# Two heads of an RWKV recurrence as one block on TensorE, and key norms repeated by transposes

## Chip, cores and metric

The kernel runs on one core of one Trainium2 chip. The metric is the device time of one execution in microseconds (us); lower is better. All arithmetic is in float32; the large products split each operand into a high and a low float32r part and add three products.

## What is computed

One residual block of a streaming encoder on 1024 frames of width 1024: half a SwiGLU feed-forward network (FFN 1, hidden width 2816), a mixing layer of two head groups, and half of FFN 2, each after an RMS norm that is scaled and shifted by a modulation vector (`silu(c) @ w_ada + b_ada`). The mixing layer projects each frame; group A (8 heads of 64) is the RWKV-7 recurrence, group B (8 heads of 64) is attention of 64-frame chunks over a band of nine chunks. Both outputs go through `w_out`.

The recurrence, per head and frame (state is 64 x 64):

```
sa    = state @ (-kk)                     # kk: the removal key, k * k_k, divided by its norm
state = state * w + sa (x) (kk * a) + v (x) k
y     = state @ r
```

The kernel computes it in chunks of 64 frames: inside a chunk the frame-to-frame dependence is a triangular system, whose inverse (TT) is computed ahead; between chunks only the state passes on.

## The kernel before

The frames are two halves (A, B) of 512. Everything is issued by a planner at build time: tasks are Python generators that say what they wait for, and a model clock of the engines decides which task issues its next instructions. Products of the large matrices ("mains") have the lowest priority and fill TensorE whenever no background task is ready; their weights are streamed through four staging buffers (`wst`), split by ScalarE (`whi`) and VectorE (`wlo`). The order of the mains is: FFN 1 of A, projection of A, FFN 1 of B, output projection of A (`oA`, which needs the recurrence rA and the attention of A), projection of B, FFN 2 of A, output projection of B, FFN 2 of B. The recurrence and attention of A run as background beside FFN 1 of B, those of B beside FFN 2 of A.

`spawn_rwkv` (L1549) makes, for a half, two groups of two head pairs. Each group is one task that prepares its two pairs one after the other (`rwkv1`, L1203) and then inverts their triangles (`inverse`, L1363); then the two recurrences (`rwkv2`, L1386) run as two tasks beside each other. The second group starts when both recurrences of the first are done.

`rwkv1` loads the shifted projections (`shift`), makes decay products `gp` and their inverse `gi`, the norms `rk` of the removal keys per head and frame, and spreads these norms over channels: L1259 to L1262 multiply a broadcast column of `rk` with the identity, eight matmuls into 64-row halves of a bank (`rkb`). It builds `RA` (r and -kk with decays) and `BKB` (kk*a, k and again kk*a, with inverse decays; head 1 reads its last two, so that head 1 has its rows in swapped order), the masked products `GA` and `GR`, and `BKn`, the transposed `BKB`. `GA`, `GR` and `BKn` are one tile per head, in the sixteen slots of the half's set, which at other times hold the normalised input.

`rwkv2` first finishes the inverse (`qb`, `ub`), then goes through eight chunks (L1440). `UV` (per head: the state's rows and the values, on opposite halves of the partitions for the two heads) is loaded ahead of it. Each chunk has three TensorE steps, each of two matmuls with 64 moving columns, one for each head: `px` (L1444), `pu` (L1454) and `pz` (L1461). VectorE copies `X` out of `px`; ScalarE and VectorE copy `pu` into `UV`, one head each; VectorE adds `pz` to the decayed state, twice 64 rows into the next chunk's `UV` and once 128 rows into `Z`. After the chunks `yb` gives the outputs, which are normalised per head, gated, transposed (`tb`) and written to `mix`, from where the output projection reads them as `mx` (L1579).

In the trace every matmul has line L512, every transpose L516 and every other recorded operation L172 (helpers), so groups are told by tile names. A float32 matmul leaves two records, a transpose one.

Of the kernel before, what the change touches and what calls it, by code (L numbers as in the profile page):

```python
# [245 lines left out]
class Builder:  # L246
# [113 lines left out]
    def setup(self):  # L360
# [3 lines left out]
        self.sets = [self.pool("set0", 16), self.pool("set1", 16)]  # L364
# [54 lines left out]
    def setup2(self):  # L419
# [26 lines left out]
        for p in range(4):  # L446
            nc.gpsimd.memset(self.Zc[p], 0.0)
        dp = self.dp
# [78 lines left out]
    def ada_first(self, v):  # L527
# [5 lines left out]
        def load(i, v=v):  # L533
            q, kb = steps[i]
            n = 2 if (v, q) in ADA_PE else 2 if v or kb in (0, 3) else 3
            w[v, i] = self.tile(self.sets[1], "n1", 16, "wa", [P, 2, 256], reads=n)
            nc.sync.dma_start(w[v, i], self.a["w_ada"][v, :, 2 * kb : 2 * kb + 2, q * 256 : q * 256 + 256])
# [63 lines left out]
    def ada(self, vs):  # L601
# [5 lines left out]
        def load(i):  # L607
            v, cb, k = steps[i]
            w[i] = self.tile(self.sets[1], "n1", 16, "wa", reads=1)
            nc.sync.dma_start(w[i], self.a["w_ada"][v, :, k, cb * H : cb * H + H])  # L610
# [92 lines left out]
    def norm_first(self):  # L703
# [18 lines left out]
        for q in range(4):  # L722
# [3 lines left out]
            for d in two:  # L726
                yield scale(d), back(d), xr[d], "th"
                nh.append(self.tile(self.sets[0], "n0", 16, "nh", dt=F32R))
# [3 lines left out]
            for d in two:  # L732
                yield t[d % 2], "n0"
                nl.append(self.tile(self.sets[0], "n0", 16, "nl", dt=F32R))
                nc.vector.scalar_tensor_tensor(nl[d], xr[d], scale(d), t[d % 2], op0=OP.mult, op1=OP.subtract)
                if d == 0:
                    self.n["n1A"] = nh, nl

    def norm(self, key, hf, j, src=None):
        nc = self.nc  # L740
        s = self.sets[hf]
# [12 lines left out]
        nh, nl, vs = [], [], []  # L754
# [6 lines left out]
        def low(d):  # L761
            nc.vector.scalar_tensor_tensor(nl[d], vs[d], scale(d)[1], nh[d].bitcast(F32), op0=OP.add, op1=OP.subtract)

        def step(d, x):
            yield x, rstd, "th", f"n{hf}", lambda: 0.0 if len(self.mains) < 2 else self.clock.at["vector"]
            sc, sh = scale(d)
# [3 lines left out]
            nh.append(self.tile(s, f"n{hf}", 16, "nh", dt=F32R))  # L770
            nl.append(self.tile(s, f"n{hf}", 16, "nl", dt=F32R))
# [373 lines left out]
    def tb(self, hf, name, shape=None):  # L1145
        return self.tile(self.sets[hf], f"n{hf}", 16, name, shape)
# [56 lines left out]
    def rwkv1(self, hf, p):  # L1203
# [36 lines left out]
        rk = self.sm("rk", [P, 8], 2, reads=10)  # L1240
# [39 lines left out]
        nc.scalar.activation(BKB[:, :, 2], BKB[:, :, 0], AF.Copy)  # L1280
# [8 lines left out]
        GR, GA, BKn = [], [], []  # L1289
        for h in range(2):  # L1290
            yield f"n{hf}"
            GR.append(self.tb(hf, "GR", [P, NC, C]))
            yield f"n{hf}"
            GA.append(self.tb(hf, "GA", [P, NC, C]))
        half = [slice(0, 64), slice(64, 128)]
        for c4 in range(2):
            yield BKB, RA, self.two
            gb = [self.bank("gb", 2) for h in range(2)]
            for i in range(4):
                c = 4 * c4 + i  # L1300
                for h, s in enumerate(half):
                    self.mm(
                        gb[h][:, i * P : i * P + P],
                        BKB[s, c, h : h + 2].rearrange("p k t -> p (k t)"),
                        RA[s, c].rearrange("p k t -> p (k t)"), side=2,
                    )
            for h in range(2):
                g4 = gb[h].rearrange("p (c k t) -> p c k t", c=4, k=2)
                for k, o in ((1, GA[h]), (0, GR[h])):
# [7 lines left out]
        for c in range(NC):  # L1317
            for h, s in enumerate(half):
                self.tp_(
                    bt[h][:, c * C : c * C + C],  # L1320
                    BKB[s, c, h : h + 2].rearrange("p k t -> p (k t)"),
                    self.ident[s, s], side=2,
                )
        for h in range(2):
            yield f"n{hf}"
            BKn.append(self.tb(hf, "BKn", [P, NC, C]))
            nc.scalar.activation(BKn[h], c3(bt[h]), AF.Copy)
# [8 lines left out]
        for h in range(2):  # L1336
            yield GA[h]
            for b in range(2):
                q = h * 64 + b * 32
                w = (4 * i + 2 * h + b) * 8  # L1340
                nc.sync.dma_start(nd[w : w + 8].rearrange("c s t -> s c t"), GA[h][q : q + 32, :, b * 32 : b * 32 + 32])
        return dict(p=p, RA=RA, GR=GR, GA=GA, BKn=BKn, bon=bon, gC=gC)

    def inverse(self, hf, st):
# [26 lines left out]
        for i in range(2):  # L1371
# [3 lines left out]
            nc.gpsimd.memset(TT, 0.0)  # L1375
        yield ud
        for i in range(2):
            for h in range(2):
                for b in range(2):
# [4 lines left out]
                    )  # L1384

    def rwkv2(self, hf, st):  # L1386
        nc = self.nc
        p, RA, GR, GA, BKn, TT = (st[k] for k in ("p", "RA", "GR", "GA", "BKn", "TT"))
        cs = slice(p * P, p * P + P)

        UV = []
        vsr = self.vs[hf].rearrange("(c t) f -> t c f", t=C)
        for h in range(2):
            yield "tr"
            UV.append(self.tr("UV", [P, NC, C]))
            o = slice(64 - h * 64, 128 - h * 64)
            nc.vector.tensor_copy(UV[h][h * 64 : h * 64 + 64, 0], self.Zc[p][h * 64 : h * 64 + 64])
            nc.sync.dma_start(UV[h][o], vsr[:, :, p * P + h * C : p * P + h * C + C])

        yield TT, "tr"  # L1400
        U1 = self.tr("U1", [P, NC, 32])
        for h in range(2):
            r0 = slice(h * 64, h * 64 + 32)
            nc.vector.transpose(U1[r0], TT[r0, :, 0:32])
        yield U1, "b"
        qb = self.bank("qb", 2)
        for c in range(NC):
            for h in range(2):
                r0 = slice(h * 64, h * 64 + 32)
                r1 = slice(h * 64 + 32, h * 64 + 64)  # L1410
                self.mm(
                    qb[r1, c * 32 : c * 32 + 32], GA[h][r0, c, 32:64], U1[r0, c],
                    tile_position=(h * 64, h * 64 + 32), side=2,
                )
        yield qb
        for h in range(2):
            r1 = slice(h * 64 + 32, h * 64 + 64)
            nc.scalar.activation(U1[r1], qb[r1, 0:256].rearrange("p (c t) -> p c t", c=NC), AF.Copy)
        yield U1, TT, "b"
        ub = self.bank("ub", 2)  # L1420
        for c in range(NC):
            for h in range(2):
# [3 lines left out]
                    ub[r0, c * 32 : c * 32 + 32], U1[r1, c], TT[r1, c, 32:64],  # L1426
# [12 lines left out]
        nc.vector.tensor_copy(Z[:, 0], self.Zc[p])  # L1439
        for c in range(NC):  # L1440
            yield *GA, *UV, "b"
            px = self.bank("px")
            for h in range(2):
# [3 lines left out]
            zg = self.sm("zg", [P, C], 3, reads=3 if c + 1 < NC else 1)  # L1447
# [3 lines left out]
            pu = self.bank("pu", 2)[:, 0:C]  # L1451
            for h in range(2):
# [4 lines left out]
            yield *UV, "b"  # L1457
            pz = self.bank("pz", 3 if c + 1 < NC else 1)[:, 0:C]
            for h in range(2):
                s = slice(h * 64, h * 64 + 64)  # L1460
                self.mm(pz[s], BKn[h][:, c], UV[h][:, c])  # L1461
            for h in range(2 if c + 1 < NC else 0):
                s = slice(h * 64, h * 64 + 64)
# [3 lines left out]
        self.free(TT, *BKn)  # L1467
# [6 lines left out]
        yield Z, *UV, self.two  # L1474
# [4 lines left out]
        for h in range(2):  # L1479
            for c in range(NC):  # L1480
                self.mm(out(h, c), GR[h][:, c], UV[h][:, c], start=c < 2, stop=False, skip_group_check=True)
# [12 lines left out]
        self.free(Z, RA, *UV, *GR, *GA, st["gC"])  # L1494
# [47 lines left out]
    def rwkv(self, hf, g, st):  # L1542
        if g == 0:
            yield from self.rwkv_prep(hf)
        for i in range(2):
            st.append((yield from self.rwkv1(hf, 2 * g + i)))
        yield from self.inverse(hf, st)

    def spawn_rwkv(self, name, hf, after):  # L1549
        v = f"{name}v"  # L1550
        self.spawn(v, self.values(hf), 3, [f"v{hf}"])
        for g in range(2):
            st = []
            self.spawn(f"{name}{g}", self.rwkv(hf, g, st), 2, after)
            after = []
            for i in range(2):
                n = f"{name}{g}_{i}"
                self.spawn(n, self.late(lambda st=st, i=i: self.rwkv2(hf, st[i])), 2 + i, [f"{name}{g}", v])
                after.append(n)
        self.spawn(name, self.end_rwkv(), 2, after)  # L1560
# [18 lines left out]
    def mixed(self, key, hf):  # L1579
# [5 lines left out]
        for c in range(9):  # L1585
            if c < 8:
                yield "th"
                q.append(self.th("mx", 2))
# [4 lines left out]
            yield m, f"n{hf}"  # L1593
            hi = self.tile(self.sets[hf], f"n{hf}", 16, "mh", dt=F32R)
            lo = self.tile(self.sets[hf], f"n{hf}", 16, "ml", dt=F32R)
            nc.scalar.activation(hi, m, AF.Copy)
            nh.append(hi)
            nl.append(lo)
            yield hi
            nc.vector.tensor_sub(lo, m, hi.bitcast(F32))  # L1600

# [122 lines left out]
```

## Time and profile before

| | before |
|---|---|
| median of 3 runs | 2178.19 us (2175.65 to 2180.26) |
| profiled execution | 2181.82 us, span 2180.1 us |
| TensorE matmul, busy | 2136.9 us, 98% |
| VectorE | 1463.8 us, 67% |
| ScalarE | 897.1 us, 41% |
| GpSimd | 128.4 us, 6% |
| granted TensorE clock, mean | 0.997 of full speed |
| DMA | 316.31 MB, mean 145 GB/s |

The profile covers one execution. Busy times are unions of the recorded durations of an engine. Matmuls are pipelined, so that their durations overlap: starts in the timeline tell more than durations. "Idle before" is what an engine stood still ahead of an instruction, with what ended that.

### The profile page before, as it was taken

The numbers are of one execution on the slowest core, as the hardware profiler recorded it, in microseconds if no ns is written. First come the engines' busy times: TensorE is split into PE (matmuls) and PEld (weight loads), VectorE is DVE, ScalarE is ACT, GpSimd is POOL, SyncE is SP. The second block draws the span as 40 slices with busy tenths as digits, with TensorE's granted clock in tenths as the row PEclk, the third lists the DMA queues.
The fourth block names the chain that finished last, engine by engine and source line by source line (L and its number), as shares of the span: only waits on it lengthen the run. The fifth ranks groups of instructions, "written<-read, shape, count | busy, mean of one in ns | idle before, by whom it ended". The sixth has DMA issues, their size and how long they took to land.

```text
span 2180.1 us, 32870 instructions
## 1 busy us (share of the span) xinstructions
PE 2136.9 (98%) x11568; PEld 1718.1 (79%) x11568; DVE 1463.8 (67%) x3090; ACT 897.1 (41%) x1712; POOL 128.4 (6%) x166
## 2 busy tenths in 40 slices
PE   6999999999999999999999999999999999999999
PEld 4788887888778868877888777867786888888887
DVE  6977777744578877877864567878787664444444
ACT  4332224445555344333555555435442343222322
POOL 1000000011300000000020300001000000000000
PEclk9999999999999999999999999999999999999999
DMA  7766655435764424334645745324432554433333
GB/s 236 243 201 210 202 161 173 132 116 160 234 189 132 121 71 125 105 94 123 215 153 163 217 146 159 110 81 128 120 106 64 184 167 141 136 97 98 96 93 102
DMA packets 230853, 316.31 MB, mean 145 GB/s; under 512 B 61976, under 2 KB 97824, under 8 KB 230688
## 3 DMA queue, kind: packets, MB, share of 16 engines
q1 hardware_dynamic: 230688, 314.22, 47.7%
q8 instruction: 91, 1.49, 0.3%
q14 instruction: 74, 0.61, 0.1%
HBM read 279.52 MB, written 34.61 MB: 144 GB/s over the span
## 4 chain that ended last, share of the span: by engine, by line
PE 86%; DMA 6%; DVE 4%; ACT 2%; issue 2%; SPq 1%; POOL 0%; DVEq 0%; ACTq 0%; POOLq 0%
PE mm L512 72%; PE mmb L512 3%; PE yp L512 1%; DMA vd<-av 1%; PE tr L516 1%; PE S L512 1%; DMA kd<-kT 1%; SPq L172 1%; PE cs L516 1%; DVE wlo L172 1%; PE gb L512 1%; PE pu L512 1%; DMA wst<-in_ffn_w 1%; PE px L512 1%; PE pz L512 1%
## 5 line engine op out<-in xcount | busy, mean ns | idle before, releaser
L172 ACT ACTIVATE whi<-wst 128x512 fp32r<-128x512 f32 (+2 forms) x692 | 423.2, 613 | 840.2 <-PE mm L512 692.1
L172 DVE TENSOR_TENSOR wlo<-wst,whi 128x512 fp32r<-128x512 f32 (+2 forms) x692 | 462.3, 671 | 341.2 <-ACT whi L172 328.0
L512 PE MATMUL mm<-nh,whi 128*128 128x512 f32 x1520 | 616.7, 406 | 0.0
L512 PE MATMUL mm<-nl,whi 128*128 128x512 f32 x1520 | 594.2, 391 | 4.3 <-DVE nl L172 4.3
L512 PE MATMUL mm<-nh,wlo 128*128 128x512 f32 x1520 | 594.8, 391 | 0.0
L512 PEld LDWEIGHTS mm<-nh,wlo 128*128 128x128 f32 x1520 | 286.0, 188 | 61.4
L512 PEld LDWEIGHTS mm<-nh,whi 128*128 128x128 f32 x1520 | 286.7, 189 | 56.4 <-issue 1.9
L512 PEld LDWEIGHTS mm<-nl,whi 128*128 128x128 f32 x1520 | 286.8, 189 | 56.1 <-DVE nl L172 5.7
L512 PE MATMUL mm<-ah,whi 128*128 128x512 f32 x670 | 273.3, 408 | 2.1 <-ACT ah L172 1.2
L512 PE MATMUL mm<-al,whi 128*128 128x512 f32 x670 | 262.4, 392 | 1.5 <-DVE al L172 1.5
L512 PE MATMUL mm<-ah,wlo 128*128 128x512 f32 x670 | 262.5, 392 | 1.1 <-DVE wlo L172 1.1
L172 DVE SCALAR_TENSOR_TENSOR h<-mm,g,h 128x512 f32<-128x512 f32 x183 | 135.9, 746 | 89.6 <-PE mm L512 88.9
L512 PEld LDWEIGHTS mm<-ah,whi 128*128 128x128 f32 x670 | 126.5, 189 | 30.1 <-ACT ah L172 2.1
L512 PEld LDWEIGHTS mm<-ah,wlo 128*128 128x128 f32 x670 | 126.3, 188 | 28.6 <-DVE wlo L172 1.5
L512 PEld LDWEIGHTS mm<-al,whi 128*128 128x128 f32 x670 | 126.6, 189 | 24.8 <-DVE al L172 2.4
L172 ACT ACTIVATE E<-E,st 128x640 f32<-128x640 f32 (+4 forms) x128 | 85.8, 688 | 32.4 <-DVE st L172 32.0
L172 DVE SCALAR_TENSOR_TENSOR acc<-wa,silc,acc 128x512 f32<-128x512 f32 (+1 forms) x120 | 83.5, 705 | 0.6
L172 DVE TENSOR_TENSOR sw<-sw,mm 128x512 f32<-128x512 f32 x85 | 58.4, 687 | 35.7 <-PE mm L512 32.3
L172 ACT ACTIVATE pt<-tr 128x256 fp32r<-128x256 f32 x144 | 49.4, 344 | 65.8 <-PE tr L516 60.4
L512 PE MATMUL mm<-whi,nh 128*128 128x512 f32 x184 | 73.8, 401 | 0.0
L512 PE MATMUL mm<-wlo,nh 128*128 128x512 f32 x184 | 71.8, 390 | 0.0
L512 PE MATMUL mm<-whi,nl 128*128 128x512 f32 x184 | 71.7, 390 | 0.0
(247 smaller groups left out, 2631.3 us busy)
## 6 DMA issues: line engine op xcount, KB each, us to landing
wst<-in_ffn_w SPq DMA_DIRECT2D x468, 256.0 KB, 2.8
wa<-in_w_ada SPq DMA_DIRECT2D x144, 256.0 KB, 4.0
wst<-in_w_v SPq DMA_DIRECT2D x64, 256.0 KB, 2.9
wst<-in_ffn_w SPq DMA_DIRECT2D x64, 192.0 KB, 2.4
wst<-in_w_t SPq DMA_DIRECT2D x40, 256.0 KB, 4.1
wst<-in_w_out SPq DMA_DIRECT2D x32, 256.0 KB, 3.0
kd<-kT SPq DMA_DIRECT2D x48, 128.0 KB, 3.9
bias<-in_bias SPq DMA_DIRECT2D x16, 320.0 KB, 4.2
```

Source lines behind the costliest of these rows:

```text
L172: return f(*args, **kw)
L512: self.nc.tensor.matmul(out, lhsT, rhs, start=start, stop=stop, **kw)
L516: self.nc.tensor.transpose(out, in_, ident)
```

## The change

The matmuls of two heads are laid beside each other, so that each step of a chunk is one 128x128 matmul with 128 moving columns. `px` and `pz` take both heads' rows on the same partitions, and only their diagonal blocks are read; `X` is a block-diagonal tile whose other blocks are zeroed once at the start. `UV` of both heads lies in the tile `RA` (slots 1 and 2), whose slot 1 is copied to `GA` first, and its values are loaded by one transfer after that copy. `BKB` has two slots instead of three. `GA` and `BKn` are one double tile for both heads; the sixteen slots of each set become eight single and four double ones, of the same bytes, in all users (norms, modulation weights, `mixed`). The temporaries `tr` go from ten to eight, and `mx` is read into them. The norms are repeated over channels by one ScalarE copy into `wide` and four full transposes. The preparation of each pair is a task of its own. The core of the diff:

```diff
+        self.Xd = [cp.tile([P, P], F32, name=f"Xd{i}") for i in range(4)]
+    def slot(self, hf, name, shape=None, dt=F32, reads=None):
+        return self.tile(self.sets[hf], f"n{hf}", 8, name, shape, dt, reads)
+    def slots(self, hf, name, shape, dt=F32, reads=None):
+        return self.tile(self.sets[hf], f"d{hf}", 4, name, shape, dt, reads)
     def tr(self, name, shape=None, dt=F32, reads=None):
-        return self.tile(self.sp, "tr", 10, name, shape, dt, reads)
+        return self.tile(self.sp, "tr", 8, name, shape, dt, reads)
...
-        yield rk, "b", "tr"
+        yield rk, "tr"
+        wide = self.tr("wide", [P, 4, 2, C])
+        nc.scalar.activation(wide, rk.rearrange("p (q h) -> p q h", h=2).unsqueeze(3).to_broadcast([P, 4, 2, C]), AF.Copy)
+        yield wide, "b", "tr"
         rb = self.bank("rkb")
         for q in range(4):
-            for h in range(2):
-                w = rk[:, 2 * q + h : 2 * q + h + 1].to_broadcast([P, C])
-                self.mm(rb[h * 64 : h * 64 + 64, q * P : q * P + P], w, self.ident)
+            self.tp_(rb[:, q * P : q * P + P], wide[:, q].rearrange("p h c -> p (h c)"), self.ident)
...
-        RA = self.sm("RA", [P, NC, 2, C], 2)
+        RA = self.sm("RA", [P, NC, 3, C], 2)
...
+        self.done.add(f"RA{hf}{p}")
         yield RA, "BKB"
-        BKB = self.sm("BKB", [P, NC, 3, C], 1)
+        BKB = self.sm("BKB", [P, NC, 2, C], 1)
...
-        nc.scalar.activation(BKB[:, :, 2], BKB[:, :, 0], AF.Copy)
...
-        nc.scalar.activation(GA[0][0:64], RA[0:64, :, 1], AF.Copy)
-        nc.gpsimd.tensor_copy(GA[1][64:128], RA[64:128, :, 1])
+        for h, s in enumerate(heads):
+            nc.scalar.activation(GA[0:64, :, h], RA[s, :, 1], AF.Copy)
+        yield GA
+        UV = RA[:, :, 1:3]
+        for h, s in enumerate(heads):
+            nc.vector.tensor_copy(UV[0:64, 0, h], self.Zc[p][s])
+        nc.sync.dma_start(
+            UV[64:128].rearrange("p c h v -> p c (h v)"), vsr[:, :, cs]
+        )
...
         for c in range(NC):
...
-                self.mm(px[h * 64 : h * 64 + 64, 0:C], GA[h][:, c], UV[h][:, c], skip_group_check=True)
-            X = self.sm("X", [P, C], 4, reads=2)
-            nc.vector.tensor_copy(X, px[:, 0:C])
+            self.mm(px[:, 0:P], hv(GA[:, c]), hv(UV[:, c]))
+            X = self.Xd[p % 2 * 2 + c % 2]
+            nc.vector.tensor_copy(X[0:64, 0:64], px[0:64, 0:64])
+            nc.scalar.activation(X[64:128, 64:128], px[64:128, 64:128], AF.Copy)
...
-                self.mm(pu[s], TT[s, c], X[s])
-            nc.scalar.activation(UV[0][0:64, c], pu[0:64], AF.Copy)
-            nc.vector.tensor_copy(UV[1][64:128, c], pu[64:128])
+            t = min(c, NC - 2) * C
+            self.mm(pu[:, 0:P], Tf[:, t : t + P], X)
+            nc.scalar.activation(hv(UV[0:64, c]), pu[heads[c == NC - 1], 0:P], AF.Copy)
...
-                self.mm(pz[s], BKn[h][:, c], UV[h][:, c])
-            for h in range(2 if c + 1 < NC else 0):
-                s = slice(h * 64, h * 64 + 64)
-                nc.vector.scalar_tensor_tensor(UV[h][s, c + 1], pz[s], gc[s], zg[s], op0=OP.mult, op1=OP.add)
-            zn = Z[:, c + 1] if c + 1 < NC else self.Zc[p]
-            nc.vector.scalar_tensor_tensor(zn, pz, gc, zg, op0=OP.mult, op1=OP.add)
+            self.mm(pz[:, 0:P], hv(BKn[:, c]), hv(UV[:, c]))
+            for h, s in enumerate(heads):
+                zn = UV[0:64, c + 1, h] if c + 1 < NC else self.Zc[p][s]
+                nc.vector.scalar_tensor_tensor(zn, pz[s, h * 64 : h * 64 + 64], gc[s], zg[s], op0=OP.mult, op1=OP.add)
+            for h, s in enumerate(heads if c + 1 < NC else []):
+                nc.scalar.activation(Z[s, c + 1], UV[0:64, c + 1, h], AF.Copy)
...
+        self.spawn(up, self.rwkv_prep(hf), 2, after)
+        before = [up, up]
         for g in range(2):
+            st = {}
+            pre = [f"{name}{g}p{i}" for i in range(2)]
+            for i in range(2):
+                x = [before[i]] + [f"RA{hf}{2 * g}"] * i
+                self.spawn(pre[i], self.late(lambda st=st, p=2 * g + i: self.rwkv1(hf, p, st)), 2, x)
+            self.spawn(f"{name}{g}", self.late(lambda st=st: self.inverse(hf, st)), 2, pre)
+            before = []
             for i in range(2):
                 n = f"{name}{g}_{i}"
                 self.spawn(n, self.late(lambda st=st, i=i: self.rwkv2(hf, st[i])), 2 + i, [f"{name}{g}", v])
+                before.append(n)
```

## Rows read from the trace of the kernel before

**Rows 1.** The page, part 1: busy us (share of the span) xinstructions of each engine.
```profile
PE 2136.9 (98%) x11568; PEld 1718.1 (79%) x11568; DVE 1463.8 (67%) x3090; ACT 897.1 (41%) x1712; POOL 128.4 (6%) x166
```

**Rows 2.** Chain of waits, its last piece: start us, us, what.
```profile
1774.41 401.93 PE mm L512 x1773
```

**Rows 3.** Tile px: count, duration ns min/median/max, first and last start us.
```profile
L512 PE MATMUL px<-UV,GA x256: 222/222/271, 763.5 to 1677.8; 128*64 128x64 f32 x128
```

**Rows 4.** Timeline of TensorE: start us, us, engine line op out<-in xcount.
```profile
1000.11 0.40 PE L512 MATMUL mm<-nh,wlo 128*128 128x512 f32 x1
1000.44 0.33 PE L512 MATMUL pu<-X,TT 64*64 64x64 f32 x4
1000.70 0.50 PE L512 MATMUL mm<-nh,whi 128*128 128x512 f32 x1
1001.03 0.40 PE L512 MATMUL mm<-nl,whi 128*128 128x512 f32 x1
```

**Rows 5.** Timeline of TensorE, two groups of one tile shape.
```profile
798.38 0.40 PE L512 MATMUL mm<-nh,wlo 128*128 128x512 f32 x1
798.70 0.34 PE L512 MATMUL pz<-UV,BKn 128*64 128x64 f32 x4
798.87 0.29 PE L512 MATMUL px<-UV,GA 128*64 128x64 f32 x4
799.09 0.50 PE L512 MATMUL mm<-nh,whi 128*128 128x512 f32 x1
799.42 0.39 PE L512 MATMUL mm<-nl,whi 128*128 128x512 f32 x1
```

**Rows 6.** Timeline of TensorE, four full-array float32 matmuls.
```profile
1010.61 0.39 PE L512 MATMUL mm<-nh,wlo 128*128 128x512 f32 x1
1010.84 1.05 PE L512 MATMUL gate<-wu,sgd 128*128 128x128 f32 x8
1011.65 0.48 PE L512 MATMUL mm<-nh,whi 128*128 128x512 f32 x1
1011.96 0.40 PE L512 MATMUL mm<-nl,whi 128*128 128x512 f32 x1
```

**Rows 7.** Timeline of TensorE, the norms of two successive preparations.
```profile
642.27 1.09 PE L512 MATMUL rkb<-ident,rk 128*64 128x128 f32 x16
...
677.19 0.40 PE L512 MATMUL mm<-nh,wlo 128*128 128x512 f32 x1
677.52 1.09 PE L512 MATMUL rkb<-ident,rk 128*64 128x128 f32 x16
678.54 0.50 PE L512 MATMUL mm<-nh,whi 128*128 128x512 f32 x1
678.88 0.40 PE L512 MATMUL mm<-nl,whi 128*128 128x512 f32 x1
```

**Rows 8.** Timeline of TensorE, four full transposes.
```profile
672.60 0.40 PE L512 MATMUL mm<-nh,wlo 128*128 128x512 f32 x1
672.84 0.60 PE L516 MATMUL cs<-ident,sq 128*128 128x128 f32 x4
673.19 0.48 PE L512 MATMUL mm<-nh,whi 128*128 128x512 f32 x1
673.51 0.40 PE L512 MATMUL mm<-nl,whi 128*128 128x512 f32 x1
```

**Rows 9.** Tiles pu and pz: durations of two VectorE operations.
```profile
L172 DVE COPY UV<-pu x64: 220/228/231, 766.3 to 1679.5; 64x64 f32<-64x64 f32 x64
...
L172 DVE SCALAR_TENSOR_TENSOR Z<-pz,gC,zg x56: 282/284/286, 769.2 to 1676.9; 128x64 f32<-128x64 f32 x56
```

**Rows 10.** DMA issues: count, KB each, median us from issue to landing.
```profile
UV<-vs SPq DMA_DIRECT2D x16, 128.0 KB, 3.1
```

**Rows 11.** Tile mh: when the output projection's input is made and first used.
```profile
L512 PE MATMUL mm<-mh,whi x128: 389/389/478, 1047.3 to 1766.1; 128*128 128x512 f32 x128
L172 ACT ACTIVATE mh<-mx x16: 612/626/636, 1027.9 to 1712.8; 128x512 fp32r<-128x512 f32 x16
```

More of the change, by code (lines that the diff above doesn't have):

```diff
@@ L363, in setup @@
         self.wp = self.pool("wp", 4)
-        self.sets = [self.pool("set0", 16), self.pool("set1", 16)]
+        self.sets = [self.pool("set0", 8), self.pool("set1", 8)]
         self.apool = self.pool("apool", 4)
@@ L447, in setup2 @@
             nc.gpsimd.memset(self.Zc[p], 0.0)
+        self.Xd = [cp.tile([P, P], F32, name=f"Xd{i}") for i in range(4)]
+        for x in self.Xd:
+            nc.gpsimd.memset(x, 0.0)
         dp = self.dp
@@ L535, in load @@
             n = 2 if (v, q) in ADA_PE else 2 if v or kb in (0, 3) else 3
-            w[v, i] = self.tile(self.sets[1], "n1", 16, "wa", [P, 2, 256], reads=n)
+            if v == 0:
+                w[v, i] = self.slot(1, "wa", [P, 2, 256], reads=n)
+            else:
+                if i % 2 == 0:
+                    w["two"] = self.slots(1, "wa", [P, 2, 2, 256], F32, reads=2 * n)
+                w[v, i] = w["two"][:, i % 2]
             nc.sync.dma_start(w[v, i], self.a["w_ada"][v, :, 2 * kb : 2 * kb + 2, q * 256 : q * 256 + 256])
@@ L608, in load @@
             v, cb, k = steps[i]
-            w[i] = self.tile(self.sets[1], "n1", 16, "wa", reads=1)
+            w[i] = self.slot(1, "wa", reads=1)
             nc.sync.dma_start(w[i], self.a["w_ada"][v, :, k, cb * H : cb * H + H])
@@ L727, in norm_first @@
                 yield scale(d), back(d), xr[d], "th"
-                nh.append(self.tile(self.sets[0], "n0", 16, "nh", dt=F32R))
+                nh.append(self.slot(0, "nh", dt=F32R))
                 nc.scalar.activation(nh[d], xr[d], AF.Identity, bias=shift(d), scale=scale(d))
@@ L732, in norm_first @@
             for d in two:
-                yield t[d % 2], "n0"
-                nl.append(self.tile(self.sets[0], "n0", 16, "nl", dt=F32R))
-                nc.vector.scalar_tensor_tensor(nl[d], xr[d], scale(d), t[d % 2], op0=OP.mult, op1=OP.subtract)
+                if d % 2 == 0:
+                    yield t[d % 2], "d0"
+                    lows = self.slots(0, "nl", [P, 2, H], F32R)
+                yield t[d % 2]
+                nc.vector.scalar_tensor_tensor(lows[:, d % 2], xr[d], scale(d), t[d % 2], op0=OP.mult, op1=OP.subtract)
+                nl.append(lows[:, d % 2])
                 if d == 0:
@@ L761, in low @@
         def low(d):
-            nc.vector.scalar_tensor_tensor(nl[d], vs[d], scale(d)[1], nh[d].bitcast(F32), op0=OP.add, op1=OP.subtract)
+            o = lows[d // 2][:, d % 2]
+            nc.vector.scalar_tensor_tensor(o, vs[d], scale(d)[1], nh[d].bitcast(F32), op0=OP.add, op1=OP.subtract)
+            nl.append(o)
         def step(d, x):
             yield x, rstd, "th", f"n{hf}", lambda: 0.0 if len(self.mains) < 2 else self.clock.at["vector"]
+            if d % 2 == 0:
+                yield f"d{hf}"
+                lows.append(self.slots(hf, "nl", [P, 2, H], F32R))
             sc, sh = scale(d)
@@ L769, in step @@
             vs.append(v)
-            nh.append(self.tile(s, f"n{hf}", 16, "nh", dt=F32R))
-            nl.append(self.tile(s, f"n{hf}", 16, "nl", dt=F32R))
+            nh.append(self.slot(hf, "nh", dt=F32R))
             nc.scalar.activation(nh[d], v, AF.Identity, bias=sh)
@@ L1145, in tb @@
     def tb(self, hf, name, shape=None):
-        return self.tile(self.sets[hf], f"n{hf}", 16, name, shape)
+        return self.slot(hf, name, shape)
     def shift(self, i, hf):
@@ L1287, in rwkv1 @@
         self.free(rs)
-        GR, GA, BKn = [], [], []
+        GR = []
         for h in range(2):
@@ L1292, in rwkv1 @@
             GR.append(self.tb(hf, "GR", [P, NC, C]))
-            yield f"n{hf}"
-            GA.append(self.tb(hf, "GA", [P, NC, C]))
+        yield f"d{hf}"
+        GA = self.slots(hf, "GA", [P, NC, 2, C])
         half = [slice(0, 64), slice(64, 128)]
@@ L1303, in rwkv1 @@
                         gb[h][:, i * P : i * P + P],
-                        BKB[s, c, h : h + 2].rearrange("p k t -> p (k t)"),
-                        RA[s, c].rearrange("p k t -> p (k t)"), side=2,
+                        BKB[s, c].rearrange("p k t -> p (k t)"),
+                        RA[s, c, 0:2].rearrange("p k t -> p (k t)"), side=2,
                     )
@@ L1308, in rwkv1 @@
                 g4 = gb[h].rearrange("p (c k t) -> p c k t", c=4, k=2)
-                for k, o in ((1, GA[h]), (0, GR[h])):
+                for k, o in ((1, GA[:, :, h]), (0, GR[h])):
                     nc.vector.tensor_mul(
@@ L1320, in rwkv1 @@
                     bt[h][:, c * C : c * C + C],
-                    BKB[s, c, h : h + 2].rearrange("p k t -> p (k t)"),
+                    BKB[s, c].rearrange("p k t -> p (k t)"),
                     self.ident[s, s], side=2,
                 )
+        yield f"d{hf}"
+        BKn = self.slots(hf, "BKn", [P, NC, 2, C])
         for h in range(2):
-            yield f"n{hf}"
-            BKn.append(self.tb(hf, "BKn", [P, NC, C]))
-            nc.scalar.activation(BKn[h], c3(bt[h]), AF.Copy)
+            yield bt[h]
+            nc.scalar.activation(BKn[:, :, h], c3(bt[h]), AF.Copy)
         self.free(BKB)
@@ L1336, in rwkv1 @@
         for h in range(2):
-            yield GA[h]
+            yield GA
             for b in range(2):
-                q = h * 64 + b * 32
+                q = b * 32
                 w = (4 * i + 2 * h + b) * 8
-                nc.sync.dma_start(nd[w : w + 8].rearrange("c s t -> s c t"), GA[h][q : q + 32, :, b * 32 : b * 32 + 32])
-        return dict(p=p, RA=RA, GR=GR, GA=GA, BKn=BKn, bon=bon, gC=gC)
+                nc.sync.dma_start(nd[w : w + 8].rearrange("c s t -> s c t"), GA[q : q + 32, :, h, q : q + 32])
+        st[p % 2] = dict(p=p, RA=RA, GR=GR, GA=GA, BKn=BKn, bon=bon, gC=gC)
     def inverse(self, hf, st):
@@ L1375, in inverse @@
             nc.gpsimd.memset(TT, 0.0)
+            yield "tr"
+            st[i]["T1"] = self.tr("T1", [32, NC, 32], reads=1)
         yield ud
@@ L1384, in inverse @@
                     )
+            w = (4 * i + 2) * 8
+            nc.sync.dma_start(st[i]["T1"], ud[w : w + 8].rearrange("c s t -> s c t"))
     def rwkv2(self, hf, st):
         nc = self.nc
-        p, RA, GR, GA, BKn, TT = (st[k] for k in ("p", "RA", "GR", "GA", "BKn", "TT"))
+        p, RA, GR, GA, BKn, TT, T1 = (st[k] for k in ("p", "RA", "GR", "GA", "BKn", "TT", "T1"))
         cs = slice(p * P, p * P + P)
[L1391 to L1404, printed above, removed]
+        heads = [slice(0, 64), slice(64, 128)]
+        hv = lambda t: t.rearrange("p h v -> p (h v)")
+        yield TT, T1, "tr"
+        U1 = self.tr("U1", [P, 2, NC, 32])
+        nc.vector.transpose(U1[0:32, 0], TT[0:32, :, 0:32])
+        nc.vector.transpose(U1[0:32, 1], T1)
         yield U1, "b"
@@ L1408, in rwkv2 @@
             for h in range(2):
-                r0 = slice(h * 64, h * 64 + 32)
                 r1 = slice(h * 64 + 32, h * 64 + 64)
                 self.mm(
-                    qb[r1, c * 32 : c * 32 + 32], GA[h][r0, c, 32:64], U1[r0, c],
-                    tile_position=(h * 64, h * 64 + 32), side=2,
+                    qb[r1, c * 32 : c * 32 + 32], GA[0:32, c, h, 32:64], U1[0:32, h, c],
+                    tile_position=(0, h * 64 + 32), side=2,
                 )
@@ L1450, in rwkv2 @@
             yield X, TT, "b"
-            pu = self.bank("pu", 2)[:, 0:C]
-            for h in range(2):
-                s = slice(h * 64, h * 64 + 64)
-                self.mm(pu[s], TT[s, c], X[s])
-            nc.scalar.activation(UV[0][0:64, c], pu[0:64], AF.Copy)
-            nc.vector.tensor_copy(UV[1][64:128, c], pu[64:128])
[L1457 to L1460, printed above, removed]
-                self.mm(pz[s], BKn[h][:, c], UV[h][:, c])
-            for h in range(2 if c + 1 < NC else 0):
-                s = slice(h * 64, h * 64 + 64)
-                nc.vector.scalar_tensor_tensor(UV[h][s, c + 1], pz[s], gc[s], zg[s], op0=OP.mult, op1=OP.add)
-            zn = Z[:, c + 1] if c + 1 < NC else self.Zc[p]
-            nc.vector.scalar_tensor_tensor(zn, pz, gc, zg, op0=OP.mult, op1=OP.add)
-        self.free(TT, *BKn)
+            pu = self.bank("pu", 1)
+            t = min(c, NC - 2) * C
+            self.mm(pu[:, 0:P], Tf[:, t : t + P], X)
+            nc.scalar.activation(hv(UV[0:64, c]), pu[heads[c == NC - 1], 0:P], AF.Copy)
+            yield BKn, UV, "b"
+            pz = self.bank("pz", 2)
+            self.mm(pz[:, 0:P], hv(BKn[:, c]), hv(UV[:, c]))
[4 more added lines that the diff above has]
+                nc.scalar.activation(Z[s, c + 1], UV[0:64, c + 1, h], AF.Copy)
+        self.free(TT, BKn)
         yield "tr", "sm", "wu"
@@ L1473, in rwkv2 @@
         sm = self.sm("sm", [P, 4, 4, 2], 2)
-        yield Z, *UV, self.two
+        yield Z, UV, self.two
         yb = [self.bank("yb", 2) for h in range(2)]
@@ L1480, in rwkv2 @@
             for c in range(NC):
-                self.mm(out(h, c), GR[h][:, c], UV[h][:, c], start=c < 2, stop=False, skip_group_check=True)
+                self.mm(out(h, c), GR[h][:, c], UV[:, c, h], start=c < 2, stop=False, skip_group_check=True)
         for c in range(NC):
@@ L1540, in rwkv2 @@
         nc.sync.dma_start(self.mix[hf][p], yo)
[L1542 to L1547, printed above, removed]
     def spawn_rwkv(self, name, hf, after):
-        v = f"{name}v"
+        v, up = f"{name}v", f"{name}p"
         self.spawn(v, self.values(hf), 3, [f"v{hf}"])
+        self.spawn(up, self.rwkv_prep(hf), 2, after)
+        before = [up, up]
         for g in range(2):
-            st = []
-            self.spawn(f"{name}{g}", self.rwkv(hf, g, st), 2, after)
-            after = []
+            st = {}
[5 more added lines that the diff above has]
+            before = []
             for i in range(2):
@@ L1558, in spawn_rwkv @@
                 self.spawn(n, self.late(lambda st=st, i=i: self.rwkv2(hf, st[i])), 2 + i, [f"{name}{g}", v])
-                after.append(n)
-        self.spawn(name, self.end_rwkv(), 2, after)
+                before.append(n)
+        self.spawn(name, self.end_rwkv(), 2, before)
     def end_rwkv(self):
@@ L1592, in mixed @@
             m = q.popleft()
-            yield m, f"n{hf}"
-            hi = self.tile(self.sets[hf], f"n{hf}", 16, "mh", dt=F32R)
-            lo = self.tile(self.sets[hf], f"n{hf}", 16, "ml", dt=F32R)
+            yield m, f"n{hf}", *([] if len(nh) % 2 else [f"d{hf}"])
+            hi = self.slot(hf, "mh", dt=F32R)
+            if len(nh) % 2 == 0:
+                two = self.slots(hf, "ml", [P, 2, H], F32R)
+            lo = two[:, len(nh) % 2]
             nc.scalar.activation(hi, m, AF.Copy)
             nh.append(hi)
-            nl.append(lo)
             yield hi
             nc.vector.tensor_sub(lo, m, hi.bitcast(F32))
+            nl.append(lo)
     def wout(self, key, hf):
```

28 lines of the change are left out of this document (15 added, 13 removed).

## The prediction

> **What bounds the kernel now.** I read the page's busy times first: TensorE is busy 2136.9 of 2180.1 us, VectorE 67%, ScalarE 41% [rows 1]. Then the chain of waits, to see what the busy engine does at the end: its last piece is 1773 product matmuls back to back in 401.93 us, 0.2267 us each [rows 2]. The work that the change touches lies wholly before that piece (the first and last recurrence matmuls start at 763.5 and 1677.8 us, [rows 3]) and runs as a background beside the products of FFN 1 of half B and FFN 2 of half A. So TensorE's own time is the bound, and an edit is worth what it takes out of TensorE's queue; work on the other engines counts only if TensorE comes to wait for it. Third, I read TensorE's timeline around the background groups, because their listed durations overlap and say little. What a group costs is the start of the second product behind it, less the start of the last product ahead of it, less two pitches of 0.2267.
>
> **The recurrence, TensorE.** There are 8 runs (4 head pairs, 2 halves) of 8 chunks with three steps px, pu, pz: 192 groups of four records (256 records for each step, [rows 3]). Before, a group is two matmuls of 64 columns on part of the array; after, it is one 128x128 matmul with 128 moving columns.
> - One group alone among products, pu: 1000.11 to 1001.03 is 0.92, less 0.453: 0.467 us [rows 4].
> - Two groups of one tile shape, pz and px (128x64): 798.38 to 799.42 is 1.04, less 0.453: 0.587 us [rows 5]. The second group adds 0.120. So the arithmetic of a group is 0.120 and the rest of a lone group, 0.347, is entering and leaving its tile shape: 0.174 for each change of shape.
> - Four full-array float32 matmuls with 128 moving columns (gate): 1010.61 to 1011.96 is 1.35, less 0.453: 0.897, so 0.224 each, with no change of shape [rows 6]. That is the new group.
>
> Along the whole timeline I count 390 changes of tile shape between consecutive TensorE records; with px, pu and pz at full shape 112 are left. So 278 x 0.174 = 48.4 us go, and 192 x (0.224 - 0.120) = 20.0 us come: **28.4 us** saved. Bounds: were each group alone, 192 x (0.467 - 0.224) = 46.7 us; were all in pairs of one shape, 96 x (0.587 - 0.448) = 13.3 us. I take the count of changes, which lies between.
>
> Here a rule of the Trainium skill speaks against the change. TensorEngine Tiling (Array Packing), section "Theoretical Speedup", holds that matrices with a dimension of 64 or less gain up to twofold from tiles, so filling the array with a block-diagonal X loses; the rows agree on the arithmetic (0.120 against 0.224). The same page, section "Key Properties", says that a change of tiling mode drains the engine, without a price; the rows put 0.174 us on it. By the first rule alone the sum would be a loss of 20 us; with both it is the gain above.
>
> **The norms over channels, TensorE.** Eight broadcast matmuls (16 records) in 64-column tiles become four transposes. Before: 677.19 to 678.88 is 1.69, less 0.453: 1.237 us [rows 7]. Four full transposes (cs): 672.60 to 673.51 is 0.91, less 0.453: 0.457 us [rows 8]. Eight preparations: 8 x 0.78 = **6.2 us** saved.
>
> **VectorE and ScalarE.** Per chunk VectorE loses one copy of UV (228 ns) and the 128-row update of Z (284 ns) [rows 9]: 64 x 0.51 = 33 us less in all. ScalarE gains half of X and two copies of Z per chunk, about 3 x 0.23 at the price of the copy in [rows 9]: 64 x 0.69 = 44 us more, and eight wide copies of the norms against eight BKB copies that go. I cost both at nothing: TensorE's products hide them, and ScalarE idles 59% of the span. Were the cover gone, that is, were every step of the recurrence late by one extra copy, it would be up to 192 x 0.23 = 44 us; I keep that as an end for the waits, with 0 as the other (less latency is as possible as more: per chunk VectorE has four operations for six). I take 2 us.
>
> **UV's load.** UV moves into RA, so its transfer (one instead of two per run) can be issued only after the two copies of GA, where it was issued ahead of the inverse's blocks. It takes a median 3.1 us from issue to landing [rows 10], so some 3.1 us and the copies' wait enter each recurrence's start. Behind it on SyncE's queue stand weight loads. Four staging buffers hold 4 x 12 products, 48 x 0.2267 = 10.9 us of work for TensorE [rows 2], so the delay is hidden: 0, between 0 and 8 x 3.1 = 25 us if nothing covered it.
>
> **Preparation by pairs.** The same instructions are issued, TT's blocks get one more small transfer per pair, and nothing of it is on TensorE's queue. The second pair of a group starts when the first has written RA rather than when it is done, and the next group's first pair waits for one recurrence rather than for two. What matters is when rA ends, because the output projection of half A needs it: the first piece of its input is converted at 1027.9 and its first product runs at 1047.3 [rows 11], so the chain has 19 us to spare. Half of the saving, about 17 us, brings the end of FFN 1 of half B forward and leaves 2 us; two starts of a recurrence with UV's load take about 2 x 4. Against that stands the overlap: one preparation follows the other by 35 us (642.27 to 677.52, [rows 7]), and of that a quarter to a half should go in each of two groups. I take it that the chain keeps up. The smaller pools (ten slots of temporaries become eight) I price inside the rival below; the split of the sixteen normalised tiles into eight single and four double slots holds the same bytes, and I take 0 for it, within a few us either way at the start, where TensorE waits for the modulation weights.
>
> **Sum.** 28.4 + 6.2 - 2 = 32.6 us off the profiled execution: a span of 2147.5. That execution took 2181.8 with 1.7 us around the span, 3.6 us above the median of the three runs, 2178.2. Off that median: **2145 us**.
>
> **Rivals.**
> - *The chain of half A becomes late.* With eight temporaries for two preparations and two recurrences, a preparation may wait for slots until its neighbour is done. If the overlap then gives nothing, rA comes 17 + 8 - 19 = 6 us late and TensorE idles for it: 2151. If a group loses a further half preparation, 2 x 17 us more: 2185. For it: fewer slots; against it: UV leaves that pool, which frees two slots per recurrence. It decides from the point at which mx is read after the last product of FFN 1 of half B.
> - *New waits in the recurrence eat the gain.* A lone px group today shows no wait beyond its changes of shape; if each step now waits 0.17 us for ScalarE, 192 x 0.17 = 33 us return and the time is 2178, no change. For it: X now needs two engines. Against it: ScalarE is the emptier one.
> - *Slower: full tiles cost their arithmetic and the changes of shape stay.* If a change of shape costs nothing by itself, and the lone group's 0.347 us is only the pipeline's fill behind any short group, each of 192 groups is 0.104 us dearer: 2178.2 + 20.0 - 6.2 = 2192. It decides below 20.0/278 = 72 ns per change. Against it: gate and cs, also short groups, show no such 0.347. In the Trainium skill, TensorEngine Tiling (Array Packing), "Theoretical Speedup" is the rule that, taken alone, would bring this about.
> - *More than forecast.* All groups alone, and stalls that the background causes now going with it: 46.7 + 6.2 = 53 us, 2125.
>
> **How the numbers follow.** Forecast 0.72; late chain 0.11, mostly still below 2174; waits 0.05; full tiles dearer 0.03; more 0.09. The measurement can tell 0.2%, about 4.4 us, from no change. The forecast's own range is 2158 (13.3 + 6.2 saved) to 2125; the late chain and part of the waits widen the upper side: 2126 to 2163. Faster: the forecast, "more" and nine tenths of the late chain, 0.91; same 0.05; slower 0.04, from the full tiles and the worst of the late chain.
>
> **What would show it.** In the new trace a lone px, pu or pz group should have two records of 128x128 and cost 0.22 to 0.24 us by the method above. The norms should be four transposes at about 0.45 us. The last piece of pure products should keep 0.2267 us each and start some 33 us earlier. mx should be read before the last product of FFN 1 of half B. I am wrong if lone groups still cost 0.4, if idle time stands before px, pu or pz with ScalarE or VectorE as its end, or if TensorE idles ahead of the first product of the output projection.

## The result, and the profile after

The changed kernel takes 2151.88 us (four runs, 2150.73 to 2152.34) against 2179.23: ratio 0.9873, 95% interval 0.9853 to 0.9892. Beside the first group of experiments it ran again, four times: 2149.55, ratio 0.9858 (0.9843 to 0.9872). So 27 to 31 us went; 2145 was forecast, 2126 to 2163 as the range. The profiled span fell from 2180.1 to 2148.7.

The page's busy line, against [rows 1]: TensorE is as full as before, with 480 records fewer; VectorE has 23 us less, ScalarE 50 more.

```profile
PE 2108.6 (98%) x11088; PEld 1727.5 (80%) x11088; DVE 1440.6 (67%) x2978; ACT 946.9 (44%) x1896; POOL 126.9 (6%) x162
```

The chain's last piece, against [rows 2], is the same 401.93 us and starts 31.4 us earlier, so everything was won ahead of it.

```profile
1743.00 401.93 PE mm L523 x1773
```

TensorE's timeline around a lone pu, pz and px group (start, duration, what), against [rows 4]. From the last product ahead of a group to the second behind it: 0.92 - 0.453 would be the old price. Now pu takes 0.68 - 0.453 = 0.23 and pz 0.69 - 0.453 = 0.24 us, as forecast; but this px takes 0.79 - 0.453 = 0.34.

```profile
772.97 0.39 PE L523 MATMUL mm<-nh,wlo 128*128 128x512 f32 x1
773.20 0.38 PE L523 MATMUL pu<-Xd,TT 128*128 128x128 f32 x2
773.34 0.48 PE L523 MATMUL mm<-nh,whi 128*128 128x512 f32 x1
773.65 0.40 PE L523 MATMUL mm<-nl,whi 128*128 128x512 f32 x1
...
786.79 0.39 PE L523 MATMUL mm<-nh,wlo 128*128 128x512 f32 x1
787.03 0.38 PE L523 MATMUL pz<-RA,BKn 128*128 128x128 f32 x2
787.16 0.47 PE L523 MATMUL mm<-nh,whi 128*128 128x512 f32 x1
787.48 0.39 PE L523 MATMUL mm<-nl,whi 128*128 128x512 f32 x1
...
952.15 0.40 PE L523 MATMUL mm<-nh,wlo 128*128 128x512 f32 x1
952.41 0.46 PE L523 MATMUL px<-RA,GA 128*128 128x128 f32 x2
952.63 0.48 PE L523 MATMUL mm<-nh,whi 128*128 128x512 f32 x1
952.94 0.39 PE L523 MATMUL mm<-nl,whi 128*128 128x512 f32 x1
```

Of the 26 px groups that stand alone (two records, products before and behind), the median is 0.33 and the least 0.23. What px reads last is the second of VectorE's two updates of UV; in a listing of all engines they end at 952.27 (0.60 us from 951.67), and px starts at 952.41:

```profile
951.67 0.60 DVE L172 SCALAR_TENSOR_TENSOR RA<-pz,gC,zg 64x64 f32<-64x64 f32 x2 [0.41 <-PE pz L523]
...
952.41 0.46 PE L523 MATMUL px<-RA,GA 128*128 128x128 f32 x2
```

The cost of a group, reckoned in this way, summed over all groups that hold nothing but px, pu and pz: before, 81 groups with 121 of the 192 steps cost 47.0 us, 0.388 a step; now 82 groups with 119 steps cost 33.1 us, 0.278 a step and not 0.224. So these groups cost 6.5 us more than at 0.224 each, and most of that (4 us) stands in groups with a px. Taken for all 192 steps, 0.110 less a step is an estimate of 21 us.

The norms, against [rows 7]: four transposes, 0.90 - 0.453 = 0.45 us.

```profile
853.42 0.39 PE L523 MATMUL mm<-nh,wlo 128*128 128x512 f32 x1
853.65 0.60 PE L527 MATMUL rkb<-ident,wide 128*128 128x128 f32 x4
854.00 0.47 PE L523 MATMUL mm<-nh,whi 128*128 128x512 f32 x1
854.32 0.39 PE L523 MATMUL mm<-nl,whi 128*128 128x512 f32 x1
```

Tile mh, against [rows 11]: the output projection's input is there at 1006.4 and used at 1034.9, 28 us ahead, where it was 19.

```profile
L523 PE MATMUL mm<-mh,whi x128: 389/389/478, 1034.9 to 1734.7; 128*128 128x512 f32 x128
L172 ACT ACTIVATE mh<-mx x16: 615/632/636, 1006.4 to 1685.5; 128x512 fp32r<-128x512 f32 x16
```

Changes of tile shape between consecutive TensorE records fell from 390 to 100.

### The profile page after: what moved, and what is told of

It is laid out like the page before. It is cut to its first block, busy times and chain, and to the rows that moved or that the text cites. A ratio compares the mean times of both kernels' runs of the same rounds, so it can differ in the third digit from the quotient of the medians.

```text
span 2148.7 us, 31990 instructions
## 1 busy us (share of the span) xinstructions
PE 2108.6 (98%) x11088; PEld 1727.5 (80%) x11088; DVE 1440.6 (67%) x2978; ACT 946.9 (44%) x1896; POOL 126.9 (6%) x162
## 4 chain that ended last, share of the span: by engine, by line
PE 89%; DMA 4%; DVE 3%; ACT 2%; issue 1%; SPq 1%; DVEq 0%; ACTq 0%
PE mm L523 73%; PE mmb L523 3%; PE yp L523 1%; PE S L523 1%; PE tr L527 1%; DMA kd<-kT 1%; PE px L523 1%; DVE wlo L172 1%; PE cs L527 1%; PE pz L523 1%; SPq L172 1%; PE pu L523 1%; PE gb L523 1%; PE yb L523 1%; PE row L523 1%
## 5 line engine op out<-in xcount | busy, mean ns | idle before, releaser
L172 ACT ACTIVATE ah<-sw 128x512 fp32r<-128x512 f32 x88 | 55.4, 629 | 37.3 <-DVE sw L172 37.2
```

The lines of the kernel that those rows point to most:

```text
L172: return f(*args, **kw)
```

## The experiments

Theory: TensorE is the bound, and the gain is the changes of tile shape that went. Rivals: the gain is the preparation by pairs, or the shorter chain of waits. Differences below are those of the ratios to the kernel before, times 2180 us. A difference of two ratios is good to 4 or 5 us by their intervals (the changed kernel alone gave 0.9873 and 0.9858, 3 us apart), and every edit also makes the planner place the tasks anew. Parts of a few us are therefore not resolved.

**The changed kernel again.** 

> The changed kernel as it is, beside the others on one chip, so that their times can be set against it: 2152 us by its four runs so far.


Ratio 0.9858, the level that the other runs of the changed kernel are set against.

**pu in a narrow tile.**
```diff
-            t = min(c, NC - 2) * C
-            self.mm(pu[:, 0:P], Tf[:, t : t + P], X)
-            nc.scalar.activation(hv(UV[0:64, c]), pu[heads[c == NC - 1], 0:P], AF.Copy)
+            self.mm(pu[0:64, 0:P], Tf[:, c * C : c * C + C], X)
+            nc.scalar.activation(hv(UV[0:64, c]), pu[0:64, 0:P], AF.Copy)
```


> The changed kernel, but step pu multiplies only the 64 columns of TT that are used, in a 128x64 tile; everything else is as it was, and the result is the same. Theory (a change of tile shape costs 0.174 us): each of 64 groups loses arithmetic (0.224 to 0.111 us) and gains two changes of shape (0.348), 64 x 0.235 = +15 us over the changed kernel. Rival (only arithmetic counts): 64 x (0.111 - 0.224) = -7 us.


0.9942 (0.9924 to 0.9959): +18 us. The same number of records, half as wide, and slower. TensorE's timeline in it, a lone pu and two pu together:

```profile
789.01 0.40 PE L523 MATMUL mm<-nh,wlo 128*128 128x512 f32 x1
789.34 0.43 PE L523 MATMUL pu<-Xd,TT 128*64 128x128 f32 x2
789.70 0.50 PE L523 MATMUL mm<-nh,whi 128*128 128x512 f32 x1
790.03 0.39 PE L523 MATMUL mm<-nl,whi 128*128 128x512 f32 x1
...
984.71 0.40 PE L523 MATMUL mm<-nh,wlo 128*128 128x512 f32 x1
985.03 0.65 PE L523 MATMUL pu<-Xd,TT 128*64 128x128 f32 x4
985.61 0.50 PE L523 MATMUL mm<-nh,whi 128*128 128x512 f32 x1
985.95 0.40 PE L523 MATMUL mm<-nl,whi 128*128 128x512 f32 x1
```

1.02 - 0.453 = 0.567 alone, 1.24 - 0.453 = 0.787 for two: the second adds 0.22, and the change into and out of the shape is 0.35, twice the 0.174 of the prediction. My 0.111 for the arithmetic was wrong: a narrow matmul costs as much here (0.22) as a full one (0.224), with nothing in the other half of the array. The trace has 203 changes of shape for 100, and 103 x 0.174 = 18 us: the measured time.

**All three steps in narrow tiles.**
```diff
-            self.mm(px[:, 0:P], hv(GA[:, c]), hv(UV[:, c]))
+            for h in range(2):
+                self.mm(px[h * 64 : h * 64 + 64, h * 64 : h * 64 + 64], GA[:, c, h], UV[:, c, h], skip_group_check=True)
...
-            self.mm(pz[:, 0:P], hv(BKn[:, c]), hv(UV[:, c]))
+            for h in range(2):
+                self.mm(pz[h * 64 : h * 64 + 64, h * 64 : h * 64 + 64], BKn[:, c, h], UV[:, c, h], skip_group_check=True)
```
(and pu as above) 

> The changed kernel, but all three steps of a chunk in 64-column tiles: px and pz as two matmuls of 64 moving columns, one for each head, pu as in the narrow run. Operands, copies, loads and the order of tasks stay as in the change. Theory: the 28 us that the recurrence brought go back, +28 us over the changed kernel (20 to 45, by how many groups stand alone). Rival (the gain came from the preparation by pairs, the fewer VectorE operations or the single load of UV): within 5 us of the changed kernel. Rival (only arithmetic counts): -20 us.


0.9960 (0.9942 to 0.9979): +22 us, two thirds and more of the gain back with loads, copies and pairing untouched; neither rival carries the main part. The trace has 364 changes of shape; 264 x 0.174 less 128 x 0.104 for px and pz would be 33 us. A part of the missing 11 us is seen at px: a lone px costs 0.474 here again, 0.14 over the 0.33 of the full tile and not 0.25, since the change of shape hides the wait for UV that the full tile shows. Over the 26 lone px groups of the changed kernel that is 3 us; the rest was not located.

**px twice.**
```diff
             self.mm(px[:, 0:P], hv(GA[:, c]), hv(UV[:, c]))
+            self.mm(px[:, 0:P], hv(GA[:, c]), hv(UV[:, c]))
```


> The changed kernel with each px matmul issued twice into the same place, so that 64 full-array matmuls of 128 moving columns are added. Theory (TensorE's own time is the bound): 64 x 0.224 = +14 us over the changed kernel. Rival (the recurrence runs in gaps of TensorE that the chain of waits leaves anyway): under 4 us.


0.9940 (0.9926 to 0.9955): +18 us, where 14 were expected: what is added to TensorE's queue is paid in full.

**The norms spread as before, in the changed kernel.** (The diff of the norms, reversed.) 

> The changed kernel with the norms spread as before, by eight broadcast matmuls into 64-column tiles. Theory: 8 x 0.78 = +6 us over the changed kernel (2152). Rival (the norms' chain is hidden, only its latency moved): 0 within 2 us.


0.9871 (0.9857 to 0.9884): +3 us, within the interval of both 0 and 6. Inconclusive; the order of tasks changed with it, and lone px groups have a median of 0.24 in its trace where they had 0.33.

**The norms alone, in the kernel before.** (That part of the diff alone.) 

> The kernel before with the norms alone changed: one ScalarE copy and four transposes. Theory: -6 us against the kernel before. Rival (the extra copy makes the preparation later and gives it back): 0 or slower.


0.9965 (0.9951 to 0.9978): -8 us. Tile mh shows what was nearly lost:

```profile
L512 PE MATMUL mm<-mh,whi x128: 388/389/604, 1040.9 to 1762.5; 128*128 128x512 f32 x128
L172 ACT ACTIVATE mh<-mx x16: 616/632/636, 1033.5 to 1714.7; 128x512 fp32r<-128x512 f32 x16
```

FFN 1 of B ends 6 us earlier, the chain of rA 6 us later, and the 192 products of the output projection, which take 44.9 us in the kernel before, take 50.7. So the 8 us are not the norms' 6.2 alone: with 6 lost here, some 7 more were won elsewhere in this run, and where was not found.

**Preparations in turn, in the changed kernel.**
```diff
-                x = [before[i]] + [f"RA{hf}{2 * g}"] * i
+                x = [pre[0]] if i else before
```


> The changed kernel with the preparations in turn: the second pair of a group starts when the first is done, the next group when both recurrences are. Theory (TensorE is the bound, and the changed kernel's output projection has its input 28 us ahead of the end of FFN 1 of half B): 0 to +3 us over the changed kernel, and mx is read some 25 us later. Rival (the preparation by pairs carries a part of the gain): +5 us or more.


1.0028 (1.0016 to 1.0039): +37 us over the changed kernel, slower than the kernel before. The theory's number fell. TensorE's timeline at the end of FFN 1 of B:

```profile
1040.55 0.39 PE L523 MATMUL mm<-ah,wlo 128*128 128x512 f32 x1
1048.02 1.09 PE L527 MATMUL tb<-ident,D 128*128 128x128 f32 x4 [7.08 <-DVE D L172]
1048.90 1.06 PE L527 MATMUL cs<-ident,ssq 128*128 128x128 f32 x4
1052.03 2.07 PE L523 MATMUL rb<-ident,rs 128*128 128x128 f32 x8 [2.07 <-POOL rs L172]
1057.43 0.79 PE L523 MATMUL mm<-mh,whi 128*128 128x512 f32 x1 [3.33 <-ACT whi L172]
```

The products are used up at 1040.8 while rA still normalises its last pair (tb at 1048.0); the output projection starts at 1057.4, 16.6 us later. The engine having idled, the granted clock is at its lower level (1.2 GHz) for 30.7 us from 1044.5 on; the stages' table (window; its length, busy us of PE, PEld, DVE, ACT, POOL; clock, DMA) has it, and the products of the output projection take 55.5 us instead of 44.9:

```profile
1040.00:1090.00 50.00, 33.82 (x113) 23.65 (x112) 35.44 (x55) 21.20 (x35) 3.09 (x3) 0.69 0.56 186
```

The late start and the slower products are some 27 us of the 39 by which this profile's span is longer; the rest was not taken apart. Tile mh starts at 1054.7, 48 us later than with the pairing. It is also 27 later than in the kernel before, which prepares in turn as well: the rest of the change lengthens the chain.

**px later.**
```diff
-            yield GA, UV, "b"
+            yield GA, UV, "b", lambda: self.clock.ready(UV) + 0.15
```


> The changed kernel with px issued 0.15 us later on the planner's clock, since the trace shows lone px groups at 0.33 us where pu and pz take 0.23. Theory (TensorE waits there for the second VectorE update of UV, which takes 0.28 us and which the planner thinks shorter): 0.1 us of most of 64 groups goes, -3 to -6 us against the changed kernel. Rival (the extra is not a wait but the price of px): 0.


0.9854 (0.9840 to 0.9867): -1 us, with an uncertainty of 4: not told from 0, nor from the least of the 3 to 6 expected. Lone px groups do fall to 0.23 us, but the time isn't seen to follow; waits of other groups rise (two pu together: median 0.50, where 0.45 is the least). That px waits is shown; that 3 to 6 us could be had there is not.

**The pairing alone, in the kernel before.** (That part of the diff alone: own tasks, `RA` announced.) 

> The kernel before with the preparation by pairs alone: each pair its own task, the second starting when the first has written RA, the next group's pairs when one recurrence is done. Theory (the pairing only shortens the chain of rA, which in the kernel before ended 19 us ahead of its use, so TensorE has no less to do): 0 within 3 us, with the first mh some 20 to 40 us earlier than 1028. Rival (the pairing carries the gain by itself): -20 us or more.


0.9967 (0.9957 to 0.9977): -7 us. mh is made at 1004.2, 24 us earlier, as expected; but the 7 us are more than the theory's 0 and far from the rival's 20. TensorE's longest waits in the stretch of FFN 2 of half A (us in total, times, longest), first the kernel before (1270 to 1773), then the pairing alone (1265 to 1761):

```profile
PE yp L512 <- DVE pt L172: 2.2, 3, 1.4
PE mm L512 <- DVE wlo L172: 1.1, 1, 1.1
PE mm L512 <- DVE al L172: 1.0, 2, 0.6
PE mm L512 <- DVE sw L172: 0.9, 1, 0.9
PE tb L516 <- DVE D L172: 0.8, 2, 0.6
PE gb L512 <- DVE BKB L172: 0.8, 1, 0.8
```
```profile
PE yp L512 <- DVE pt L172: 2.0, 2, 1.7
PE pz L512 <- DVE UV L172: 0.3, 1, 0.3
PE tr L516 <- DVE D L172: 0.3, 1, 0.3
PE pu L512 <- DVE X L172: 0.3, 1, 0.3
```

The waits of products for VectorE (wlo, al, sw) are gone there. From ScalarE's last copy of projection B to the first product of the next output projection it is 6.7 us shorter (452.5 to 445.8), and TensorE's idle time in that stretch falls from 7.4 to 3.1 us. So in these two profiles 4 us are waits. Why pairing brings VectorE's work in a better order isn't tested.

**Eight temporaries, in the kernel before.**
```diff
-        return self.tile(self.sp, "tr", 10, name, shape, dt, reads)
+        return self.tile(self.sp, "tr", 8, name, shape, dt, reads)
```


> The kernel before with eight temporaries instead of ten. Theory (the slots lengthen the chain of preparation and recurrence, which is why the changed kernel with preparations in turn starved TensorE): the first mh some 10 to 25 us later than 1028, the time 0 to +10 us, positive as far as TensorE then idles before the output projection. Rival (the late load of UV alone lengthens the chain): mh within 4 us of 1028, the time unchanged.


0.9999 (0.9990 to 1.0009): no change; mh at 1032.0, 4 us later. The slots alone are not the 27 us. In the trace of the preparations in turn some 7 and 5 us of it lie between qb and the first px of its two groups (12.3 and 9.4 us for 5.5 and 4.9 before), where the new copies of GA and UV's load stand; the rest lies in the preparations and was not taken apart.

**px twice, in the kernel before.** (The loop over heads runs twice.) 

> The kernel before with each px product issued twice in the same tile shape: 64 more groups of two 64-column matmuls, without a change of shape more. Theory (inside one shape two heads in two column tiles cost 0.120 us a group): 64 x 0.120 = +8 us. Rival (a group costs 0.347 us whatever stands beside it): 64 x 0.47 = +30 us.


1.0021 (1.0012 to 1.0030): +5 us. Inside one shape 64 groups more are cheap. A px group of eight records alone, in TensorE's timeline, costs 1.04 - 0.453 = 0.59, 0.12 more than the lone four:

```profile
763.07 0.40 PE L512 MATMUL mm<-nh,wlo 128*128 128x512 f32 x1
763.39 0.45 PE L512 MATMUL px<-UV,GA 128*64 128x64 f32 x8
763.78 0.50 PE L512 MATMUL mm<-nh,whi 128*128 128x512 f32 x1
764.11 0.39 PE L512 MATMUL mm<-nl,whi 128*128 128x512 f32 x1
```

The order came out with 372 changes of shape for 390, which is 3 of the 8 us.

**Norms and pairing, in the kernel before.** 

> The kernel before with the norms by transposes and the preparation by pairs, the recurrence as before. Theory: the norms' -6 us without the wait before the output projection that the norms alone showed (its products took 51 us there instead of 45): -8 to -14 us against the kernel before. Rival (the pairing adds nothing to the norms): as the norms alone, -8 us, with the output projection's products at 51 us again.


0.9950 (0.9937 to 0.9963): -11 us, with the output projection's products back at 44.9. From here to the changed kernel only the block form and what it brings with it is missing: 0.9950 to 0.9858, 20 us.

## Why the prediction was right, point by point

- *TensorE is the bound.* Right: px twice costs 18 us, and the last piece kept its 401.93 us.
- *The recurrence, 28.4 us less 2 for waits.* The mechanism is right: 0.174 us for a change of shape came out again as half of 0.35 in the narrow pu, and full groups without a wait cost 0.23. The size was too large: 20 us from norms and pairing to the whole change, 22 back when the tiles were narrow, 21 by the count of the groups. The step that was mis-sized is the 2 us for waits. The groups of px, pu and pz alone cost 6.5 us over the 0.224 that I took, with 119 of the 192 steps in them. At a lone px, 0.11 over, it is seen why: the full tile comes earlier to two VectorE updates that still take 0.28 us each. "A lone px group shows no wait beyond its changes of shape" was true and misleading: the changes hid it. So the rival of new waits came about in part, at some 0.05 us a step for its 0.17. That the time would come back if these waits went is not shown: with px later the lone ones went, and the time stayed.
- *The norms, 6.2 us.* Rows as forecast (0.45 for 1.24). In time 8 us alone (with 6 lost and 7 won elsewhere), 4 beside the pairing, 3 (inconclusive) in reverse: 6.2 is not contradicted, and no run measures it closely.
- *Preparation by pairs, 0.* Mis-sized twice. It takes 7 us by itself, some 4 of them as waits that go beside FFN 2 of half A. And it carries the rest: without it the change is slower than the kernel before. I had put the chain 6 us late without the overlap, 2151, and 2185 with a further half preparation per group, which makes it 40 late. The run without the overlap gave 2186.4, but that 2185 meets it is luck: the output projection started 16.6 us after the last product, 10.6 came from the lower clock of an engine that had idled, which I had left out, and the rest is open. For the overlap I had taken 18 to 35 us in two groups; mh moved by 24 in the kernel before and by 48 in the changed one.
- *UV's load, 0 on TensorE.* One wait of TensorE for it stands in the trace, a px of 0.4 us. In the chain it counts: from qb to the first px of half A's groups it takes 8.4 and 9.4 us, where it took 5.5 and 4.9, and the pairing had to make that good.
- *The slower rival* (changes of shape cost nothing) is refuted by the narrow pu: fewer columns, +18 us.
- *The sum* (which gives 2145.6) forecast 32.6 us less, and 27 to 31 went. The parts were further off than the whole: 26.4 was forecast for the recurrence with its waits and 20 came, 6.2 for norms and pairing together and 11 came. That these two errors cancel is luck.

## What to carry to other kernels

Where TensorE is full, a short product between long ones costs its own time and twice the change of tile shape; count the changes along the timeline and price one by a lone group against two together. The price held here, and the new steps still cost 0.278 us and not the 0.224 of the tightest rows. A saving on the full engine also brings forward the moment at which it needs the background's result: shorten that chain in the same edit, or the engine idles and the clock adds to it, as with the preparations in turn. A wait that a slower step hid appears when the step gets faster, so leave room for it in the sum.

## What was not expected of the hardware

A matmul of 64 columns by 128 moving columns took 0.22 us beside another of the same tile, as long as one of 128 columns (0.224). Two 64-column matmuls of 64 moving columns on the two halves of the array took 0.120 together. So the narrow form saved here only where both halves ran at once.
